# Two layers of a hybrid diffusion backbone: the feed-forward output is summed without its gate, and attention's results are divided by the row sums

## The chip, the core and the metric

The kernel runs on one core of a Trainium2 chip. The core has five engines that work side by side, each through its own queue of instructions: TensorE (matrix products, "PE" in the profile, with its weight loads as "PEld"), VectorE ("DVE"), ScalarE ("ACT"), GpSimd ("POOL") and SyncE ("SP"), which here only issues transfers between the chip's DRAM and the working memory SBUF. Matrix products are written to PSUM, a small memory of eight banks of 128 x 512 fp32. The metric is the device time of one execution in microseconds; lower is better.

## The reference

Two layers act on 128 context tokens and 512 latent tokens of width 1024 (`D`). What matters of one layer:

```python
h = layer_norm(x) * (1 + sc1) + sh1
o = concat([ssm(h), window_attention(h), head_attention(h)]) @ w_out
x = layer_norm(ALPHA * x + g1 * o, ln1_g, ln1_b)
h = layer_norm(x) * (1 + sc2) + sh2
a, gate = split(h @ w_ffn_in)
f = (silu(a) * gate) @ w_ffn_out          # inner width 2816
x = layer_norm(ALPHA * x + g2 * f, ln2_g, ln2_b)
```

`sh`, `sc` and the gates `g1`, `g2` come from a conditioning vector through a weight `w_ada`. There is one set for context rows and one for latent rows; each is a row of 1024 numbers that is the same for all rows of its kind. Attention is softmax(q k) v: window attention has 4 heads in which each latent token sees 256 nearby keys and 128 cached ones, grouped head attention has 8 query heads on 2 key heads with 640 keys.

## The kernel before, in words

The 640 rows are five tiles of 128 (tile 0 is context). Everything is fp32. The large products are made of three products of split operands: `split` makes a high part on ScalarE (L283) and the remainder on VectorE or GpSimd (L284), and `mm3` (L311 to L313) multiplies high by high, high by low and low by high. The conditioning weights are multiplied at L381.

The program is written in a framework that places every instruction. Each engine, and SyncE's one queue of transfers too, works strictly in the order of its own list. That order is laid out when the kernel is built, from the order of the source text and a modelled timeline; waits between engines are semaphores. Buffers come from named pools with a fixed number of slots: `k4` has 10 slots of 128 x 1024, `zt` has 2 of 128 x 512, and of PSUM there are two banks each for the names `psT` and `psM` and two double banks for `psS`. A transfer that waits for a slot, or for its data, holds back all transfers behind it in SyncE's queue.

*Head attention* (`gqa_units`) has, per layer, 2 key heads x 4 latent tiles x 2 pairs of query heads: 16 units (32 in all), besides the context tile. A unit has a front and a back. The front makes scores in a double bank (L1149), finds their maximum on VectorE (L1152, then times the scale, L1153), takes the exponential with its row sums on ScalarE (L1156), the reciprocal of the sums (L1158), and multiplies the 128 x 640 weights by it, on VectorE (L1160, 16 times) or GpSimd (L1162, 48 times). The back transposes the weights through `psT` (L852), copies them out (L1175), multiplies them with the values into the third `psT` bank, two heads on the two halves of the partitions (L1180), and copies the result (L1185). The front of one unit is written ahead of the back of the unit before, and pieces of other work (projections, the state-space model) are put between.

*Window attention* (`na_units`) is alike with 4 latent units per head pair, 16 in all, on 384 keys; the scaling is on VectorE 8 times and on GpSimd 24 times (L954), the value products are L976, and two backs lie behind the fronts.

*Output projection* (`wout`) handles the tiles in the groups (2, 1, 0) and (3, 4). For each tile it gates and adds the result to the old rows, which lie in a `k4` slot `xs[i]`, normalises them (`post_ln`, whose last VectorE operation is L1291), normalises again and prepares the feed-forward operands. `xs[i]` then holds the rows that the feed-forward result will be added to.

*Feed-forward* (`ffn`): the 22 blocks of 128 inner columns go in six parts of 4, 4, 4, 3, 4 and 3 blocks. For each block `ffn_in` forms seven products of 320 columns and sums them on VectorE (L1629), with weights prepared by L1579. After the blocks of a part, ten products of 128 x 512 (two column halves n, five tiles i) are made over the part's blocks, in `psM` and `psT` in turn, and summed into `xs[i]`:

```python
g = row("gp", M["gates"][1, 0]) if i == 0 else row("gs", M["gates"][1, 1])
t = ps
V.tensor_tensor(out=t, in0=ps, in1=g[:, cs], op=ALU.mult)            # L1746
```

followed in the first part by `xs = ALPHA * xs + t`, in the later ones by `xs = xs + t` (L1753), in the last with a running row sum (`residual`, L1296). The two gate rows are loaded to `k4` slots (L406) at the start of the feed-forward stage. Beside the blocks run side jobs: modulation weights of the next layer (`ada`, transfers `ev` from `w_ada`) and tables of its state-space model (`ssm_tables`, which hold further `k4` slots). After the last part the rows are normalised and, in the first layer, stored to DRAM as `xmid` (L1778).

Of the kernel before, what the change touches and what calls it, by code (L numbers as in the profile page):

```python
# [8 lines left out]
F32 = mybir.dt.float32  # L9
# [3 lines left out]
ALU = mybir.AluOpType  # L13
# [3 lines left out]
D = 1024  # L17
# [140 lines left out]
class Build:  # L158
# [689 lines left out]

    def transpose_to(self, pt, srcs):

        for j, s in enumerate(srcs):
            self.nc.tensor.transpose(pt[:, j * 128:(j + 1) * 128], s, self.ident)  # L852
# [46 lines left out]
    def na_units(self, l, N, mh, ml):  # L899
# [26 lines left out]
        def front(cb):  # L926
# [23 lines left out]
            for hh in range(2):  # L950
                if self.SCN[l][hh]:
                    V.tensor_scalar(out=P[:, hh], in0=P[:, hh], scalar1=sm[:, hh:hh + 1], scalar2=None, op0=ALU.mult)
                else:
                    G.tensor_tensor(out=P[:, hh], in0=P[:, hh], in1=sm[:, hh:hh + 1].broadcast_to([128, 384]),  # L954
                                    op=ALU.mult)
            return P

        def back(cb, P):
# [8 lines left out]
            for j in range(3):  # L967
                for hh in range(2):
# [5 lines left out]
                    else:  # L974
                        vt = vsh[:, (cb - 1) + j, hd]
                    nc.tensor.matmul(pt[hh * 64:hh * 64 + 64, 256:384], lhsT=vt, rhs=PT[:, j, hh],  # L976
                                     start=(j == 0), stop=(j == 2), tile_position=(0, hh * 64))
            a = slice(128 + cb * 128, 256 + cb * 128)
# [112 lines left out]
    def gqa_units(self, l, kv, zq, K, ss, mixd):  # L1091
# [47 lines left out]
        def front(a):  # L1139
            i, pr = a  # L1140
            qT = prepare(i)
            Ps = []
            for hh in range(2):
# [3 lines left out]
                for b in range(2):  # L1147
                    for kx, st, en in ((K["kH"], True, False), (K["kL"], False, True)):
                        nc.tensor.matmul(sp[:, b, 0:320], lhsT=qT[:, h * 128:(h + 1) * 128],  # L1149
                                         rhs=kx[kv][:, b * 320:(b + 1) * 320], start=st, stop=en)  # L1150
                nm = self.small(1, tag="gm", bufs=4)
                V.tensor_reduce(out=nm, in_=sp[:, :, 0:320], axis=AX.XY, op=ALU.max, negate=True)  # L1152
                V.tensor_tensor(out=nm, in0=nm, in1=sch, op=ALU.mult)  # L1153
                P = self.ys(n=640)
                sm = self.small(1, tag="gs", bufs=4)
                S.activation(P.rearrange("p (b k) -> p b k", b=2), sp[:, :, 0:320], AF.Exp, bias=nm, scale=sch,  # L1156
                             accum_out=sm)
                V.reciprocal(sm, sm)  # L1158
                if self.SCG[l][hh]:
                    V.tensor_scalar(out=P, in0=P, scalar1=sm, scalar2=None, op0=ALU.mult)  # L1160
                else:
                    G.tensor_tensor(out=P, in0=P, in1=sm.broadcast_to([128, 640]), op=ALU.mult)  # L1162
                Ps.append(P)
            return Ps

        def back(a, Ps):
            i, pr = a
            PT5 = self.b5()
# [16 lines left out]
            S.copy(outs[i][:, pr * 128:(pr + 1) * 128], pt[:, 256:384])  # L1185
# [256 lines left out]
    SCG = ((0, 0), (1, 0))  # L1442
    SCN = ((0, 0), (0, 1))
# [10 lines left out]
    def wout(self, l, M, mx, xsrc, nxt):  # L1454
# [6 lines left out]
        ada = self.ada_side(l, M, nxt)  # L1461
        self.function(AF.Silu, self.after)
# [7 lines left out]
        for group in self.GROUPS:  # L1470
# [23 lines left out]
            for i in group:  # L1494
# [5 lines left out]
                self.normalise(xs[i], xn, self.stats_of(xs[i], s, junk, "lsn"), self.NORMV[2])  # L1500
# [394 lines left out]
```

## Time and profile before

| | |
|---|---|
| median of 3 runs | 1859.57 us (1850.95 to 1860.01) |
| profiled execution | 1860.72 us |
| its span, first to last instruction | 1858.9 us |
| TensorE busy, share of the span | 1694.2 us, 91% |
| VectorE | 1257.5 us, 68% |
| GpSimd | 847.6 us, 46% |
| ScalarE | 820.5 us, 44% |
| mean granted TensorE clock | 0.927 of full speed |

Stages in the profiled execution, roughly: start and projections to 125 us; first layer's head attention to 350, window attention to 440, output projection to 575, feed-forward to 1000 and its end to 1090; second layer's head attention to 1215, window attention to 1340, output projection to 1425, feed-forward to the end.

How to read it: busy times are sums over instructions of an engine, and an engine that is not the last to finish can stand idle at no cost. [...] A wait is put down to the instruction that ended it.

### The profile page before, as it was taken

What the parts mean: (1) busy time and instruction counts of PE and PEld (TensorE: products, weight loads), DVE (VectorE), ACT (ScalarE), POOL (GpSimd) and SP (SyncE); (2) the same over time, 40 slices, a digit from 0 to 9 for tenths busy, and PEclk for the clock granted to TensorE, in tenths of its full rate; (3) what the DMA queues carried; (4) which work ended last, traced back from release to release, by engine and by line L of the source; (5) the groups of instructions that cost most, each with busy time, mean ns of one, the idle gap of its engine ahead of it and who ended that gap; (6) DMA issues with size and microseconds to landing.
All of it is one profiled execution on the core that took longest, in us unless ns stands there. A gap on an engine that the chain in (4) does not pass through costs nothing. (4 is left out here: it accounts for less than half of the span.)

```text
span 1858.9 us, 31182 instructions
## 1 busy us (share of the span) xinstructions
PE 1694.2 (91%) x11432; PEld 1474.2 (79%) x11432; DVE 1257.5 (68%) x2468; ACT 820.5 (44%) x1780; POOL 847.6 (46%) x723
## 2 busy tenths in 40 slices
PE   5889798899699999999997989999989999999997
PEld 3878577678498879798886978877768898998996
DVE  5466634744758876687978577665467776777777
ACT  5335444554633334242336556544565242433433
POOL 4755524237642616054456344211594473553553
PEclk9879998769799999999999999985889999999999
DMA  8534765535534554432414343453452222312312
GB/s 302 132 93 113 218 197 156 150 121 168 183 107 142 167 158 151 130 110 91 126 57 156 110 110 99 108 159 80 156 189 84 91 83 77 103 58 79 103 57 80
DMA packets 183113, 234.87 MB, mean 126 GB/s; under 512 B 78960, under 2 KB 112048, under 8 KB 182960
## 3 DMA queue, kind: packets, MB, share of 16 engines
q1 hardware_dynamic: 182960, 232.88, 41.0%
q8 instruction: 90, 1.47, 0.3%
q14 instruction: 63, 0.52, 0.1%
HBM read 203.57 MB, written 29.39 MB: 125 GB/s over the span
## 5 line engine op out<-in xcount | busy, mean ns | idle before, releaser
L284 POOL TENSOR_TENSOR wl<-wr,wh 128x512 fp32r<-128x512 f32 x362 | 507.8, 1423 | 464.9 <-ACT wh L283 313.4
L283 ACT CAST wh<-wr 128x512 fp32r<-128x512 f32 x450 | 275.3, 619 | 394.4 <-PE psM L313 101.7
L311 PE MATMUL psM<-hh,wh 128*128 128x320 f32 x560 | 180.1, 322 | 8.9 <-DVE modc L393 2.6
L312 PE MATMUL psM<-hl,wh 128*128 128x320 f32 x560 | 178.3, 318 | 0.0
L313 PE MATMUL psM<-hh,wl 128*128 128x320 f32 x560 | 178.1, 318 | 0.0
L311 PEld LDWEIGHTS psM<-hh,wh 128*128 128x128 f32 x560 | 109.1, 195 | 12.5 <-DVE modc L393 2.8
L1162 POOL TENSOR_TENSOR ys<-ys,sm 128x640 f32<-128x640 f32 x48 | 61.7, 1289 | 120.4 <-DVE sm L1158 89.4
L311 PE MATMUL psT<-hh,wh 128*128 128x320 f32 x352 | 109.8, 312 | 0.0
L313 PEld LDWEIGHTS psM<-hh,wl 128*128 128x128 f32 x560 | 108.7, 194 | 1.4 <-issue 1.4
L312 PEld LDWEIGHTS psM<-hl,wh 128*128 128x128 f32 x560 | 109.0, 195 | 1.0 <-issue 0.7
L313 PE MATMUL psT<-hh,wl 128*128 128x320 f32 x352 | 109.0, 310 | 0.0
L312 PE MATMUL psT<-hl,wh 128*128 128x320 f32 x352 | 108.9, 309 | 0.0
L230 POOL TENSOR_TENSOR sm<-sm,mhalf 128x1 f32<-128x1 f32 (+2 forms) x46 | 54.7, 1191 | 94.2 <-DVE sm L260 53.6
L1152 DVE TENSOR_REDUCE sm<-psS 128x1 f32<-128x640 f32 x64 | 52.0, 819 | 56.0 <-PE psS L1149 55.6
L1629 DVE TENSOR_TENSOR ys<-ys,psM 128x320 f32<-128x320 f32 x140 | 64.9, 481 | 34.8 <-PE psM L313 32.9
L1629 DVE TENSOR_TENSOR ys<-ys,psT 128x320 f32<-128x320 f32 x140 | 65.0, 481 | 30.4 <-PE psT L313 29.3
L311 PE MATMUL psT<-b,wh 128*128 128x320 f32 x240 | 76.9, 320 | 8.9 <-DVE ys L1629 8.9
L852 PE MATMUL psT<-ident,ys 128*128 128x128 f32 x440 | 79.3, 304 | 6.1 <-ACT sm L1185 2.0
L284 POOL TENSOR_TENSOR wl<-ws,wh 128x512 fp32r<-128x512 f32 x40 | 53.7, 1344 | 63.7 <-ACT wh L283 63.7
L311 PE MATMUL psM<-b,wh 128*128 128x320 f32 x240 | 76.6, 319 | 6.2 <-DVE ys L1629 6.2
L311 PE MATMUL psT<-wh,xs 128*128 128x512 f32 x190 | 75.8, 399 | 2.9 <-DVE k L1753 2.9
L311 PE MATMUL psM<-wh,xs 128*128 128x512 f32 x190 | 75.0, 395 | 2.5 <-DVE k L1753 2.5
(438 smaller groups left out, 5071.8 us busy)
## 6 DMA issues: line engine op xcount, KB each, us to landing
wr<-in_w_ffn_in_dram SPq DMA_DIRECT2D x88, 512.0 KB, 3.7
ev<-in_w_ada_dram SPq DMA_DIRECT2D x112, 256.0 KB, 3.8
wr<-in_w_ffn_out_dram SPq DMA_DIRECT2D x40, 512.0 KB, 3.9
wr<-in_w_out_dram SPq DMA_DIRECT2D x32, 512.0 KB, 3.7
wr<-in_w_in_dram SPq DMA_DIRECT2D x28, 512.0 KB, 4.4
wa<-in_w_ada_dram SPq DMA_DIRECT2D x24, 512.0 KB, 5.7
k<-in_x_dram SPq DMA_DIRECT2D x10, 512.0 KB, 5.9
xs<-zqk SPq DMA_DIRECT2D x32, 160.0 KB, 3.8
```

Source lines behind the costliest of these rows:

```text
L230: self.nc.gpsimd.tensor_tensor(out=o, in0=v, in1=self.mhalf.broadcast_to([128, v.shape[1]]), op=ALU.pow)
L283: nc.scalar.copy(hi, src)
L284: (lo_eng or nc.vector).tensor_tensor(out=lo, in0=src, in1=hi.bitcast(F32), op=ALU.subtract)
L311: nc.tensor.matmul(ps, lhsT=ah, rhs=bh, start=first, stop=False)
L312: nc.tensor.matmul(ps, lhsT=ah, rhs=bl, start=False, stop=False)
L313: nc.tensor.matmul(ps, lhsT=al, rhs=bh, start=False, stop=last)
L852: self.nc.tensor.transpose(pt[:, j * 128:(j + 1) * 128], s, self.ident)
L1152: V.tensor_reduce(out=nm, in_=sp[:, :, 0:320], axis=AX.XY, op=ALU.max, negate=True)
L1162: G.tensor_tensor(out=P, in0=P, in1=sm.broadcast_to([128, 640]), op=ALU.mult)
L1629: V.tensor_tensor(out=o, in0=x, in1=y, op=ALU.add)
```

## The change

Two things are changed, independent of each other.

*Feed-forward.* After the output projection's layer norm each tile's rows are also stored to DRAM (`xd`). The first part's products are copied into `xs[i]` by ScalarE, over the rows; the second to fourth parts are added without the gate. In the fifth part a block's rows come back from DRAM to a `zt` buffer, the product is added to the sum in PSUM, multiplied by the gate, and ALPHA times the rows is added. The sixth part is gated and added as before. The gate rows are asked for where the fifth part first uses them.

*Attention.* The weights are no longer scaled. After the value products a new helper, `over_sums`, makes two small products of the reciprocal sums (one column, broadcast to 64) with the identity, which puts them beside the result in the same PSUM bank, along the columns; the result is multiplied by them on VectorE. In window attention ScalarE first copies them to SBUF; in head attention the result is copied as before and then multiplied. In head attention both heads' sums lie in one tile with one reciprocal, and the scores' maximum is written to a free column of the scores' own bank. The context tile's softmax is as before.

```diff
+    def over_sums(self, pt, r):
+        for h in range(2):
+            self.nc.tensor.matmul(pt[64 * h:64 * h + 64, 384:512], lhsT=r[:, h:h + 1].broadcast_to([128, 64]),
+                                  rhs=self.ident, start=True, stop=True, tile_position=(0, 64 * h))
...
 # window attention, front
             V.reciprocal(sm, sm)
-            for hh in range(2):
-                if self.SCN[l][hh]:
-                    V.tensor_scalar(out=P[:, hh], in0=P[:, hh], scalar1=sm[:, hh:hh + 1], scalar2=None, op0=ALU.mult)
-                else:
-                    G.tensor_tensor(out=P[:, hh], in0=P[:, hh], in1=sm[:, hh:hh + 1].broadcast_to([128, 384]),
-                                    op=ALU.mult)
-            return P
+            return P, sm
...
 # window attention, back, after the value products
+            self.over_sums(pt, sm)
+            rb = self.zt(128)
+            S.copy(rb, pt[:, 384:512])
+            V.tensor_tensor(out=pt[:, 256:384], in0=pt[:, 256:384], in1=rb, op=ALU.mult)
             a = slice(128 + cb * 128, 256 + cb * 128)
             self.split(pt[:, 256:384], mh[:, a], ml[:, a])
...
 # head attention, front, for each of two heads
-                nm = self.small(1, tag="gm", bufs=4)
-                V.tensor_reduce(out=nm, in_=sp[:, :, 0:320], axis=AX.XY, op=ALU.max, negate=True)
-                V.tensor_tensor(out=nm, in0=nm, in1=sch, op=ALU.mult)
+                nm, m = self.small(1, tag="gm", bufs=4), sp[:, 0, 320:321]
+                V.tensor_reduce(out=m, in_=sp[:, :, 0:320], axis=AX.XY, op=ALU.max, negate=True)
+                V.tensor_tensor(out=nm, in0=m, in1=sch, op=ALU.mult)
...
-                V.reciprocal(sm, sm)
-                if self.SCG[l][hh]:
-                    V.tensor_scalar(out=P, in0=P, scalar1=sm, scalar2=None, op0=ALU.mult)
-                else:
-                    G.tensor_tensor(out=P, in0=P, in1=sm.broadcast_to([128, 640]), op=ALU.mult)
+                             accum_out=sm[:, hh:hh + 1])
                 Ps.append(P)
-            return Ps
+            V.reciprocal(sm, sm)
+            return Ps, sm
...
 # head attention, back, after the value products
-            S.copy(outs[i][:, pr * 128:(pr + 1) * 128], pt[:, 256:384])
+            self.over_sums(pt, sm)
+            o = outs[i][:, pr * 128:(pr + 1) * 128]
+            S.copy(o, pt[:, 256:384])
+            V.tensor_tensor(out=o, in0=o, in1=pt[:, 384:512], op=ALU.mult)
...
 # output projection, after a tile's layer norms
+                nc.sync.dma_start(xd[i], xs[i])
...
 # feed-forward
-        for key, cd in (("gp", 0), ("gs", 1)):
-            row(key, M["gates"][1, cd])
...
-                g = row("gp", M["gates"][1, 0]) if i == 0 else row("gs", M["gates"][1, 1])
-                t = ps
-                V.tensor_tensor(out=t, in0=ps, in1=g[:, cs], op=ALU.mult)
+                x = xs[i][:, cs]
                 if part == 0:
-                    V.scalar_tensor_tensor(out=xs[i][:, cs], in0=xs[i][:, cs], scalar=ALPHA, in1=t, op0=ALU.mult,
-                                           op1=ALU.add)
-                elif last:
-                    self.residual(xs[i][:, cs], t, sums[n])
+                    S.copy(x, ps)
+                elif part < len(PARTS) - 2:
+                    V.tensor_tensor(out=x, in0=ps, in1=x, op=ALU.add)
                 else:
-                    V.tensor_tensor(out=xs[i][:, cs], in0=xs[i][:, cs], in1=t, op=ALU.add)
+                    g = row("gp", M["gates"][1, 0]) if i == 0 else row("gs", M["gates"][1, 1])
+                    if last:
+                        V.tensor_tensor(out=ps, in0=ps, in1=g[:, cs], op=ALU.mult)
+                        self.residual(x, ps, sums[n])
+                    else:
+                        t = self.zt()
+                        nc.sync.dma_start(t, xd[i][:, cs])
+                        V.tensor_tensor(out=ps, in0=ps, in1=x, op=ALU.add)
+                        V.tensor_tensor(out=ps, in0=ps, in1=g[:, cs], op=ALU.mult)
+                        V.scalar_tensor_tensor(out=x, in0=t, scalar=ALPHA, in1=ps, op0=ALU.mult, op1=ALU.add)
```

## Rows read from the trace of the kernel before

**Rows 1.** The page's first section: busy us, share of the span, instructions.

```profile
PE 1694.2 (91%) x11432; PEld 1474.2 (79%) x11432; DVE 1257.5 (68%) x2468; ACT 820.5 (44%) x1780; POOL 847.6 (46%) x723
```

**Rows 2.** Stretches: us, then busy us of PE, PEld, DVE, ACT, POOL; granted clock.

```profile
125.00:350.00 225.00, 190.88 (x1651) 159.89 (x1651) 118.42 (x268) 103.59 (x259) 88.76 (x89) 0.88 0.57 165
...
575.00:1000.00 425.00, 407.08 (x2718) 360.60 (x2718) 328.44 (x563) 151.62 (x304) 188.40 (x142) 0.98 0.41 126
1090.00:1215.00 125.00, 119.01 (x969) 106.75 (x970) 86.41 (x204) 76.52 (x196) 46.64 (x50) 0.95 0.37 99
1215.00:1340.00 125.00, 118.36 (x636) 92.10 (x636) 68.42 (x152) 63.34 (x158) 33.83 (x36) 0.73 0.48 137
1425.00:1800.00 375.00, 367.16 (x2158) 340.71 (x2157) 276.67 (x421) 136.77 (x263) 175.77 (x130) 1.00 0.24 78
```

**Rows 3.** TensorE's waits, 575 to 1000 us: total us, times, longest.

```profile
PE psM L311 <- DVE ys L1629: 5.6, 5, 2.8
...
PE psT L311 <- DVE ys L1629: 3.1, 1, 3.1
PE psM L311 <- DVE k L1753: 2.5, 1, 2.5
```

**Rows 4.** TensorE's waits, 1425 to 1800 us.

```profile
PE psT L311 <- DVE ys L1629: 3.8, 5, 1.5
PE psT L311 <- DVE k L1753: 2.5, 1, 2.5
```

**Rows 5.** VectorE's groups by form: busy us, mean ns, idle us before, who ended it.

```profile
L1579 DVE TENSOR_TENSOR wr<-wr 128x512 f32<-128x512 f32 x40 | 48.0, 1200 | 0.7
...
L1746 DVE TENSOR_TENSOR psM<-psM,k 128x512 f32<-128x512 f32 x50 | 34.7, 695 | 26.9 <-PE psM L313 26.9
...
L1579 DVE TENSOR_TENSOR wr<-wr,wr 128x512 f32<-128x512 f32 x40 | 29.3, 732 | 0.9 <-POOL wl L284 0.7
...
L1753 DVE TENSOR_TENSOR k<-k,psM 128x512 f32<-128x512 f32 x40 | 27.2, 680 | 0.6
...
L1158 DVE RECIPROCAL sm<-sm 128x1 f32<-128x1 f32 x64 | 10.1, 158 | 30.8 <-ACT ys L1156 30.3
```

**Rows 6.** GpSimd's groups by form: the two scalings of attention.

```profile
L1162 POOL TENSOR_TENSOR ys<-ys,sm 128x640 f32<-128x640 f32 x48 | 61.7, 1289 | 120.4 <-DVE sm L1158 89.4 <-DVE sm L1153 13.5 <-DVE xs L740 8.2
...
L954 POOL TENSOR_TENSOR ys<-ys,sm 128x384 f32<-128x384 f32 x24 | 21.7, 921 | 70.0 <-DVE sm L949 67.9 <-PE psM L824 2.1
```

**Rows 7.** TensorE's groups by form.

```profile
L852 PE MATMUL psT<-ident,ys 128*128 128x128 f32 x440 | 79.3, 304 | 6.1 <-ACT sm L1185 2.0 <-ACT b L1175 1.3 <-DVE ys L847 1.2
...
L1149 PE MATMUL psS<-b,xs 128*128 128x320 f32 x256 | 54.1, 340 | 12.7 <-ACT ys L1156 10.7 <-DVE xs L1088 1.8
...
L1180 PE MATMUL psT<-b,b 128*64 128x128 f32 x640 | 44.7, 285 | 0.1
...
L381 PE MATMUL psM<-ev,silc 128*32 128x128 f32 x320 | 21.5, 351 | 22.2 <-DMA ev<-in_w_ada_dram 22.0
...
L976 PE MATMUL psT<-ys,k 128*64 128x128 f32 x128 | 12.5, 326 | 0.1
```

**Rows 8.** TensorE in order of time, fifth part of the first layer.

```profile
932.16 0.50 PE L311 MATMUL psM<-wh,xs 128*128 128x512 f32 x1 [2.49 <-DVE k L1753]
```

**Rows 9.** VectorE in order of time there: first and last of eight.

```profile
929.03 0.70 DVE L1746 TENSOR_TENSOR psM<-psM,k 128x512 f32<-128x512 f32 x1 [2.68 <-PE psM L313]
...
933.22 0.68 DVE L1753 TENSOR_TENSOR k<-k,psT 128x512 f32<-128x512 f32 x1
```

**Rows 10.** DMA issues by line: size and median us to landing.

```profile
k<-gates SPq DMA_DIRECT2D x8, 512.0 KB, 5.1
...
wr<-in_w_ffn_out_dram SPq DMA_DIRECT2D x8, 256.0 KB, 2.9
```

**Rows 11.** Waits of SyncE's DMA queue.

```profile
SPq L1778 <- DVE k L1291: 27.7, 4, 19.6
```

More of the change, by code (lines that the diff above doesn't have):

```diff
@@ L949, in front, with back @@
             V.reciprocal(sm, sm)
-            for hh in range(2):
-                if self.SCN[l][hh]:
-                    V.tensor_scalar(out=P[:, hh], in0=P[:, hh], scalar1=sm[:, hh:hh + 1], scalar2=None, op0=ALU.mult)
-                else:
-                    G.tensor_tensor(out=P[:, hh], in0=P[:, hh], in1=sm[:, hh:hh + 1].broadcast_to([128, 384]),
-                                    op=ALU.mult)
-            return P
-        def back(cb, P):
+            return P, sm
+        def back(cb, front):
+            P, sm = front
             PT = self.big("ys").rearrange("p (j h q) -> p j h q", j=3, h=2)
@@ L1141, in front @@
             qT = prepare(i)
-            Ps = []
+            Ps, sm = [], self.small(2, tag="gs", bufs=4)
             for hh in range(2):
@@ L1150, in front, with back @@
                                          rhs=kx[kv][:, b * 320:(b + 1) * 320], start=st, stop=en)
-                nm = self.small(1, tag="gm", bufs=4)
-                V.tensor_reduce(out=nm, in_=sp[:, :, 0:320], axis=AX.XY, op=ALU.max, negate=True)
-                V.tensor_tensor(out=nm, in0=nm, in1=sch, op=ALU.mult)
+                nm, m = self.small(1, tag="gm", bufs=4), sp[:, 0, 320:321]
+                V.tensor_reduce(out=m, in_=sp[:, :, 0:320], axis=AX.XY, op=ALU.max, negate=True)
+                V.tensor_tensor(out=nm, in0=m, in1=sch, op=ALU.mult)
                 P = self.ys(n=640)
-                sm = self.small(1, tag="gs", bufs=4)
                 S.activation(P.rearrange("p (b k) -> p b k", b=2), sp[:, :, 0:320], AF.Exp, bias=nm, scale=sch,
-                             accum_out=sm)
-                V.reciprocal(sm, sm)
-                if self.SCG[l][hh]:
-                    V.tensor_scalar(out=P, in0=P, scalar1=sm, scalar2=None, op0=ALU.mult)
-                else:
-                    G.tensor_tensor(out=P, in0=P, in1=sm.broadcast_to([128, 640]), op=ALU.mult)
+                             accum_out=sm[:, hh:hh + 1])
                 Ps.append(P)
-            return Ps
-        def back(a, Ps):
+            V.reciprocal(sm, sm)
+            return Ps, sm
+        def back(a, front):
             i, pr = a
+            Ps, sm = front
             PT5 = self.b5()
@@ L1441 @@
     XPOS = 1
-    SCG = ((0, 0), (1, 0))
-    SCN = ((0, 0), (0, 1))
     YR = 3
@@ L1461, in wout @@
         ada = self.ada_side(l, M, nxt)
+        xd = self.dp.tile([NT, 128, D], F32, name=self.nm("xd"))
         self.function(AF.Silu, self.after)
@@ L1500, in wout @@
                 self.normalise(xs[i], xn, self.stats_of(xs[i], s, junk, "lsn"), self.NORMV[2])
+                nc.sync.dma_start(xd[i], xs[i])
                 self.ffn_in_tile(xn, i, M["modc"], H)
-        return self.ffn(l, xs, M, H, nxt, ada)
+        return self.ffn(l, xs, xd, M, H, nxt, ada)
     LO = (True, True)
@@ L1705, in ffn_in_plain, with ffn @@
         yield gh, gl
-    def ffn(self, l, xs, M, H, nxt, ada):
+    def ffn(self, l, xs, xd, M, H, nxt, ada):
         nc, I = self.nc, self.I
```

## The prediction, made before the changed kernel was run

> **What bounds the kernel now.** Read the busy times first: TensorE is busy 1694.2 of 1858.9 us, VectorE 1257.5, GpSimd 847.6, ScalarE 820.5 [rows 1]. So the change, which mostly takes work from VectorE and GpSimd, can shorten the end only where TensorE stands still for them, and it adds work to TensorE itself. Then read the stretches [rows 2]. The first layer's head attention (125 to 350 us) leaves TensorE 34.1 us idle at a mean granted clock of 0.88; the second layer's (1090 to 1215) leaves 6.0. The second layer's window attention (1215 to 1340) is busy 118.4 of 125 us, but at a clock of 0.73. The feed-forward parts are nearly full: 407.1 of 425 us and 367.2 of 375, so 17.9 + 7.8 = 25.7 us idle there, at clocks of 0.98 and 1.00.
>
> Third, TensorE's waits inside these feed-forward stretches, to see who ends the idle time. Additions of the block products (L1629) end 5.6 + 3.1 us in the first layer and 3.8 in the second; the second half of the output's summing (L1753) ends 2.5 in each [rows 3, 4]. That is 17.5 us in which VectorE's lateness holds TensorE, and only 5.0 of it names the work that the change edits. Last, a close look at one of these: eight summing operations start on VectorE between 929.03 and 933.22 us, first four products with the gate, then four additions, so 4.19/7 = 0.60 us apart; a PSUM bank comes free only with an addition, and TensorE stood 2.49 us [rows 8, 9].
>
> **The change, part by part.** The sum is made against the profiled execution's own time of 1860.7 us (span 1858.9); the median of the runs shown is 1859.6, 1.1 lower, which is taken off at the end.
>
> *Summing ungated.* Each layer has ten output blocks in each of six parts. Before, each block costs a multiplication (695 ns) and an addition (680 ns) [rows 5]. Now the first part needs neither (ScalarE copies), the next three only the addition, the fifth three operations, the last two as before. In the first four parts that is 50 operations fewer per layer, in the fifth 10 more: 80 fewer in the two layers, at about 0.69 us 55 us of VectorE's 1257.5. ScalarE's 20 copies lie beside it, and that engine is idle over half the time [rows 1]. TensorE gets back what it waited for. The 2.5 us of the second layer [rows 4] stand outside the fifth part; four operations instead of eight free the bank 4 x 0.60 = 2.4 us sooner, so this wait goes. Of the 12.5 us that L1629 ends I take 5: those additions stand in VectorE's queue behind weight preparation and table work too, which stays. Term: -7.5, with bounds of 0 (all of it is other work's fault) and -15 (12.5 + 2.5).
>
> *The fifth part* now has three VectorE operations per block. Two things follow. Where four blocks are handled together, the bank is freed after the ninth operation or later rather than the fifth: 4 x 0.60 = 2.4 us more at the stall of [rows 8], and I charge the same once in each layer: +5. And the third operation needs 256 KB of the saved rows in one of two buffers; such a load lands 2.9 us after issue [rows 10]. Two buffers give a block every (2.9 + 0.7 + some 0.5 of queueing)/2, about 2.1 us, against four blocks' PSUM; close to the pace of the products themselves (12 matmuls of 512 columns), so I charge nothing more, but the upper bound is 20 loads with 1 us each: +25. Behind a load that waits for its buffer stand the weight loads of the next part on the same SyncE queue. The gate rows (512 KB, 5.1 us to landing [rows 10]) are asked for in the fifth part instead of at the start. Their two buffers are free earlier, so they can be issued far ahead; without that cover each layer pays 5.1 us once.
>
> *The stores of the rows.* Ten stores of 512 KB are new on SyncE's queue, each waiting for the layer norm on VectorE that makes its rows, with output weights, feed-forward weights and modulation weights queued behind. The kernel already has such a store: L1778 waits for the same operation (L1291), and the queue stood 27.7 us in four of them, 19.6 in the worst [rows 11]. TensorE already waits 22.0 us in all for modulation weights that come through this queue [rows 7]. The order of the queue is laid out from a modelled timeline, so most stores should stand near where their rows are ready. Term: +4 for both layers; bounds 0 and 27.7 x 10/4 = 69, of which the loads in flight should hide well over half.
>
> *Row sums after the values.* GpSimd loses 48 x 1289 ns and 24 x 921 ns = 84 us [rows 6], VectorE the other 24 scalings. On the path this is worth nearly nothing: the transposes that read the scaled weights come a unit later, and their idle time, 6.1 us over 440, names ScalarE and an earlier VectorE line, not GpSimd [rows 7]. What covers the removed scaling is the next unit's scores. New are two matmuls per unit, 64 + 32 = 96, of the same tile shape as the value products: 44.7/640 = 0.070 us each in head attention, 12.5/128 = 0.098 in window attention, so 64 x 0.070 + 32 x 0.098 = 7.6 us of TensorE. In the second layer it is full, in the first some falls into the idle time: +6. Bounds: 0, if the 34.1 us of idle time swallow it, and 96 x 79.3/440 = 17.3, if the broadcast column makes each cost what a full transpose does [rows 7]. The new copy and product after the values hold the transposes' second bank longer, but the next unit asks for it a unit later. One reciprocal per unit in place of two removes half of VectorE's stops for the exponential, 30.3 us [rows 5]; TensorE's wait on score banks is 10.7 us [rows 7]. The new product waits for a ScalarE copy on the same queue, which gives part of that back. Term: -3, bounds 0 and -10.7.
>
> [...] In the rows a 512-column operation takes 695 ns with an input in PSUM and 732 ns (mean) with both in SBUF [rows 5], so no surcharge shows and none is in the sum. [...]
>
> **Sum.** -7.5 + 5 + 4 + 6 - 3 = +4.5: 1865.2 by the profiled execution, 1864 by the median. The measurement of this kernel tells little under 0.5%, 9.3 us, from no change, so this is no change that can be told.
>
> **The rivals.** *Faster, VectorE was the hidden bound (0.27).* All 17.5 us named above but the fifth part's 2.5 go (-15), VectorE is far enough ahead in the fifth part to owe nothing, the stores hide, and the scores' wait falls by its whole 10.7 against +6: 1860.7 - 19.7, about 1840. For it: the waits named are real. Against: much of L1629's wait is work that stays, and TensorE's share is already over 95% there.
>
> *Attention gains from a quiet GpSimd (0.08).* Two forms of one line, L1579, of the same shape take 732 and 1200 ns [rows 5]: VectorE loses 0.47 us when something is in its way. Taking 72 GpSimd operations away could spare 72 x 0.47 = 34 us of VectorE and with it the full 10.7 us on the score banks: 7.7 less than the sum, 1856. [...]
>
> *Slower, SyncE's queue (0.15).* The stores stand where L1778 stands: a stop of 27.7/4 = 6.9 us each, a third of it felt by TensorE, ten times: 23 instead of 4, so 1883. It decides as soon as a store is placed several us before its rows are ready while a weight buffer is already free.
>
> *Slower, TensorE's added work (0.10).* The 96 matmuls cost 17.3 instead of 6, in stretches that run partly at the lower of the two clock levels: 1875.
>
> The forecast itself has 0.40; its own range is 1852 to 1874.
>
> **How the numbers follow.** Below 1850 lie the first rival and a little of the forecast's edge: faster 0.29. Above 1869 lie the two slower rivals and the forecast's upper edge: 0.15 + 0.10 + 0.04 = 0.29. The rest, 0.42, is within 0.5%. The range reaches into the first and third rival: 1842 to 1884.
>
> **What would show it.** Right: VectorE about 55 us less busy in the feed-forward parts and GpSimd about 84 less in attention, TensorE 6 to 9 us busier, no wait named by the summing addition outside the fifth part, a longer one inside it. Wrong: waits of TensorE for feed-forward or modulation weights right after the layer norms (the queue), idle time in the fifth part ended by loads of saved rows, or attention stretches that shrink or stretch by more than 10 us, above all with another granted clock.

## The result, and the profile after

The changed kernel takes 1840.24 us (median of 4 runs, 1836.5 to 1845.8) against 1859.62 for the kernel before on the same chip (4 runs): a ratio of 0.990, 95% interval 0.985 to 0.994. It is about 1% faster, below the range's lower end of 1842. Its profiled execution takes 1840.08 us with a span of 1837.9, against 1858.9. Ratios leave out runs more than 1.5% above the fastest of their kernel; the means of the experiments keep them, and without them a difference in that table would change by up to 6 us, a rest by about 1.

The first section of the page of the changed kernel, to be read beside [rows 1]:

```profile
PE 1675.5 (91%) x11624; PEld 1466.9 (80%) x11624; DVE 1181.7 (64%) x2380; ACT 833.4 (45%) x1816; POOL 763.4 (42%) x651
```

GpSimd lost 84.2 us, as worked out (84), and VectorE 75.8. But TensorE, which received 192 records more, is busy 18.7 us *less*. The groups of TensorE (busy us, mean ns, idle us before and who ended it) show the new products on the first line, and below it what [rows 7] showed before:

```profile
L852 PE MATMUL psT<-ident,sm 128*64 128x128 f32 x192 | 19.6, 282 | 0.0
...
L858 PE MATMUL psT<-ident,ys 128*128 128x128 f32 x440 | 75.2, 295 | 4.0 <-DVE sm L1189 2.3 <-DVE xs L1093 0.8 <-ACT ys L290 0.7
L1154 PE MATMUL psS<-b,xs 128*128 128x320 f32 x256 | 54.7, 345 | 8.5 <-ACT ys L1160 6.6 <-DVE xs L1093 1.8
L1181 PE MATMUL psT<-b,b 128*64 128x128 f32 x640 | 43.7, 283 | 2.0 <-ACT b L1176 1.9
```

The 96 products have 192 records in the trace, two each, and take 19.6 us, 0.204 each. So work was added, and yet the busy time fell. The windows by stage say how: the kernel before first, cut at the first scores of each kind of attention, then the changed kernel (columns as in [rows 2]; the last but two is the granted clock).

```profile
125.00:337.00 212.00, 180.13 (x1609) 152.12 (x1609) 109.51 (x245) 96.75 (x241) 88.61 (x88) 0.90 0.56 161
337.00:430.00 93.00, 88.04 (x459) 65.81 (x458) 47.63 (x115) 47.70 (x124) 31.22 (x34) 0.75 0.46 137
1086.00:1238.00 152.00, 140.26 (x1148) 124.79 (x1148) 102.98 (x231) 89.68 (x225) 53.25 (x58) 0.96 0.40 108
1238.00:1338.00 100.00, 96.80 (x454) 73.59 (x455) 51.44 (x123) 49.26 (x127) 26.41 (x27) 0.66 0.46 135
```

```profile
125.00:325.00 200.00, 173.05 (x1676) 148.60 (x1676) 101.49 (x245) 96.10 (x241) 48.52 (x56) 0.94 0.60 174
325.00:417.00 92.00, 88.33 (x477) 68.44 (x477) 46.77 (x121) 48.84 (x131) 17.16 (x18) 0.76 0.44 131
560.00:985.00 425.00, 402.53 (x2681) 358.57 (x2682) 300.07 (x504) 156.12 (x310) 184.12 (x140) 0.98 0.42 131
1076.00:1235.00 159.00, 146.27 (x1230) 130.93 (x1230) 92.47 (x225) 91.62 (x233) 34.07 (x43) 0.95 0.40 108
1235.00:1318.00 83.00, 80.24 (x458) 60.39 (x458) 43.59 (x110) 46.91 (x125) 17.15 (x18) 0.82 0.52 152
1402.00:1780.00 378.00, 372.08 (x2198) 345.16 (x2197) 258.30 (x390) 146.24 (x281) 178.27 (x132) 1.00 0.26 83
```

In these two executions two stages carry the gain. The first layer's head attention is 12 us shorter, of which 4.9 are idle time (31.9 to 27.0) and the rest goes with a clock of 0.94 instead of 0.90. The second layer's window attention is 17 us shorter without doing less: its clock is 0.82 instead of 0.66. TensorE's busy time there fell from 96.8 to 80.2 us, with 458 records for 454. Against this stand 7 us more in the second layer's head attention and 3 between the first layer's window attention and it.

Only the first of the two is stable. The changed kernel was profiled twice more (e5, span 1818.6 us; e18, 1845.0); these are its two window attentions, cut alike:

```profile
323.00:407.00 84.00, 80.67 (x476) 61.89 (x476) 46.02 (x120) 48.50 (x131) 17.17 (x18) 0.84 0.48 144
1219.00:1301.00 82.00, 79.24 (x455) 59.77 (x454) 42.73 (x108) 46.84 (x125) 17.15 (x18) 0.82 0.52 152
```

```profile
319.00:421.00 102.00, 95.51 (x476) 73.88 (x477) 46.50 (x120) 49.18 (x131) 17.15 (x18) 0.70 0.41 120
1233.00:1326.00 93.00, 90.69 (x455) 68.63 (x455) 42.38 (x107) 47.52 (x125) 17.14 (x18) 0.70 0.44 134
```

Between these two executions of one program lie 29 us in window attention alone, where the clock was lower, so a single profile can't show what the edit did to the clock of this stage. The first layer's head attention took 200, 198 and 195 us in the three.

Inside the feed-forward the terms can be read one by one. TensorE in order of time, fifth part of the first layer, as in [rows 8]:

```profile
918.54 0.80 PE L311 MATMUL psT<-wh,xs 128*128 128x512 f32 x1 [4.88 <-DVE k L1761]
```

2.49 us before, 4.88 now: the 2.4 us of four more operations. TensorE's waits in the two feed-forward stretches (560 to 985, then 1402 to 1780 us), as in [rows 3, 4]; L1633 is what L1629 was:

```profile
PE psT L311 <- DVE k L1761: 4.9, 1, 4.9
PE psM L311 <- DVE ys L1633: 4.8, 4, 2.7
PE psT L311 <- DVE ys L1633: 4.3, 2, 3.1
```

```profile
PE psT L311 <- DVE ys L1633: 2.9, 5, 0.8
PE psM L311 <- DVE ys L1633: 1.1, 1, 1.1
PE psT L311 <- DVE k L1761: 0.9, 1, 0.9
```

The second layer's 2.5 us by the summing addition are gone (0.9 is left in its fifth part). L1633 holds TensorE for 4.8 + 4.3 + 2.9 + 1.1 = 13.1 us. Before, L1629 held it 12.5 us by the lines of [rows 3, 4] and 13.9 in all, since the second layer's stretch (1425 to 1800 us) has one line more:

```profile
PE psM L311 <- DVE ys L1629: 1.4, 2, 1.1
```

VectorE's summing groups show that this work did shrink. The edited lines, of which these are some, take 96.4 us in all where they took 151.2, the 55 us less of the forecast:

```profile
L1750 DVE TENSOR_TENSOR k<-psT,k 128x512 f32<-128x512 f32 x30 | 20.7, 690 | 31.9 <-PE psT L313 31.9
L1750 DVE TENSOR_TENSOR k<-psM,k 128x512 f32<-128x512 f32 x30 | 20.7, 689 | 28.5 <-PE psM L313 28.5
...
L1761 DVE SCALAR_TENSOR_TENSOR k<-zt,psT 128x512 f32<-128x512 f32 x10 | 6.8, 682 | 2.4 <-DMA zt<-xd 2.3
```

The transfers of the saved rows (all instructions on `xd`, who waited for them, and their time to landing):

```profile
L1758 SPq DMA_DIRECT2D zt<-xd x20: 319/320/432, 485.1 to 1764.7; - x20
L1504 SPq DMA_DIRECT2D xd<-k x10: 319/326/433, 440.8 to 1383.9; - x10
its engine sat idle before it (us, times) until:
who waited for it (us, times):
  DVE k L1761: 2.3, 2
...
DMA to landing us min/median/max: 2.4/2.9/5.6
```

Twenty loads cost VectorE 2.3 us, and no engine waited for a store. SyncE's queue did stand at both, most of all

```profile
SPq L1758 <- DVE k L1761: 37.3, 16, 10.7
SPq L1504 <- DVE b L284: 11.8, 2, 6.4
```

in all 48.4 us at the loads, mostly for a `zt` buffer, and 17.4 at the stores. Little of it reached TensorE: the modulation weights `ev` that come through the same queue hold it 27.4 us (22.2 and 5.2 in two banks) for 25.8 before (22.0 and 3.8), and 24.4 in e2, which has the same stores.

### The profile page after: what moved, and what is told of

Read it like the earlier page. It is cut to its first block, busy times and chain, and to the rows that moved or that the text cites. A ratio compares the mean times of both kernels' runs of the same rounds, so it can differ in the third digit from the quotient of the medians.

```text
span 1837.9 us, 31442 instructions
## 1 busy us (share of the span) xinstructions
PE 1675.5 (91%) x11624; PEld 1466.9 (80%) x11624; DVE 1181.7 (64%) x2380; ACT 833.4 (45%) x1816; POOL 763.4 (42%) x651
## 4 chain that ended last, share of the span: by engine, by line
PE 64%; DVE 13%; DMA 11%; POOL 4%; ACT 4%; issue 3%; SPq 1%; POOLq 0%; DVEq 0%; ACTq 0%
PE psM L311 8%; PE psM L312 8%; PE psM L313 8%; PE psT L311 5%; PE psT L312 5%; PE psT L313 5%; DMA ev<-in_w_ada_dram 3%; PE psT L858 3%; POOL wl L284 2%; DMA wr<-in_w_ffn_in_dram 2%; PE psS L767 2%; PE psS L311 2%; PE psS L312 2%; PE psS L313 2%; PE psS L1154 2%
## 5 line engine op out<-in xcount | busy, mean ns | idle before, releaser
L311 PEld LDWEIGHTS psM<-hh,wh 128*128 128x128 f32 x560 | 108.1, 193 | 10.7 <-DVE modc L391 3.6
L1583 DVE TENSOR_TENSOR ws<-wr,wr 128x512 f32<-128x512 f32 x40 | 33.6, 839 | 85.8 <-DMA wr<-in_w_ffn_in_dram 54.4
L1633 DVE TENSOR_TENSOR ys<-ys,psM 128x320 f32<-128x320 f32 x140 | 64.9, 482 | 35.4 <-PE psM L313 33.5
L1157 DVE TENSOR_REDUCE psS<-psS 128x1 f32<-128x640 f32 x64 | 52.0, 826 | 54.6 <-PE psS L1154 51.8
L1633 DVE TENSOR_TENSOR ys<-ys,psT 128x320 f32<-128x320 f32 x140 | 64.9, 481 | 29.7 <-PE psT L313 28.6
L858 PE MATMUL psT<-ident,ys 128*128 128x128 f32 x440 | 75.2, 295 | 4.0 <-DVE sm L1189 2.3
L311 PE MATMUL psM<-wh,hh 128*128 128x256 f32 (+1 forms) x232 | 73.1, 315 | 5.9 <-DVE sm L1326 2.9
```

Of the source, the lines that this page charges most:

```text
L311: nc.tensor.matmul(ps, lhsT=ah, rhs=bh, start=first, stop=False)
L1157: V.tensor_reduce(out=m, in_=sp[:, :, 0:320], axis=AX.XY, op=ALU.max, negate=True)
L1583: V.tensor_tensor(out=o, in0=x, in1=y, op=op)
L1633: V.tensor_tensor(out=o, in0=x, in1=y, op=ALU.add)
```

## The experiments

Every run lists its span and TensorE's mean granted clock. In the traces this clock is 1.00 of full speed or 0.50: in windows of 2 us of the profile before, all fifteen from 370 to 400 us have 0.50 and all ten from 402 to 422 us have 1.00, and a value between the two (0.83 from 400 to 402 us) stands where a window holds a change. So the time at the lower level is twice the span times one minus the mean clock. Within one kernel, whose instructions are the same each time, the span follows the clock: over 279 runs of 18 kernels (the changed one in three sets), each set taken from its own mean, the slope is -13.3 us for +0.01 of clock (standard error 0.5, correlation -0.88). A mean clock 0.01 higher means about 37 us less at the lower level (2 x 0.01 x 1856), so each of these is worth 13.3/37 = 0.36 us. By the clock of 0.50 alone it would be at most a half, as an estimate; the runs give less, and their number is used here.

With this slope each kernel's mean difference from the kernel before is split into what goes with its clock and a rest. The split takes for granted that the slope within a kernel also holds from kernel to kernel, which no run tests. The table gives the ratio to the kernel before on the same chip, then means over all runs; the rest is good to 1 or 2 us.

| kernel | runs | ratio [95%] | span | clock | difference | by clock | rest |
|---|---|---|---|---|---|---|---|
| before, five chips | 111 | | 1855.6 | 0.929 | | | |
| changed | 4 | 0.990 [0.985, 0.994] | 1838.5 | 0.940 | -17.1 | -14.7 | -2.5 |
| changed, e5 | 6 | 0.981 [0.977, 0.986] | 1826.2 | 0.944 | -29.5 | -20.1 | -9.4 |
| changed, e18 | 9 | 0.989 [0.985, 0.992] | 1837.9 | 0.938 | -17.7 | -11.7 | -6.0 |
| e1 attention | 10 | 0.991 [0.988, 0.994] | 1837.7 | 0.939 | -17.9 | -12.7 | -5.2 |
| e2 feed-forward | 12 | 0.995 [0.992, 0.998] | 1846.3 | 0.934 | -9.3 | -6.0 | -3.3 |
| e3 window attention | 12 | 0.997 [0.994, 1.000] | 1847.3 | 0.937 | -8.4 | -10.1 | +1.8 |
| e4 head attention | 11 | 0.994 [0.990, 0.997] | 1842.4 | 0.932 | -13.2 | -4.2 | -9.1 |
| e6 window, products only | 12 | 0.995 [0.992, 0.998] | 1844.7 | 0.938 | -11.0 | -11.7 | +0.7 |
| e7 window, no scaling | 12 | 0.994 [0.992, 0.997] | 1844.5 | 0.937 | -11.1 | -10.3 | -0.8 |
| e8 changed, bank free sooner | 6 | 0.990 [0.985, 0.994] | 1838.1 | 0.941 | -17.5 | -15.0 | -2.5 |
| e9 idle operations, window | 12 | 0.999 [0.996, 1.001] | 1854.2 | 0.931 | -1.5 | -2.0 | +0.6 |
| e10 window, products 3 times | 8 | 0.991 [0.988, 0.994] | 1840.6 | 0.942 | -15.0 | -16.7 | +1.6 |
| e11 head, products only | 6 | 0.988 [0.985, 0.992] | 1835.1 | 0.942 | -20.5 | -16.3 | -4.2 |
| e12 head, no scaling | 6 | 0.978 [0.975, 0.981] | 1815.0 | 0.941 | -40.7 | -15.9 | -24.8 |
| e13 idle operations, head | 6 | 0.990 [0.986, 0.994] | 1843.9 | 0.928 | -11.7 | +1.9 | -13.5 |
| e14 idle operations x3, window | 12 | 1.001 [0.998, 1.004] | 1856.9 | 0.928 | +1.3 | +1.2 | +0.1 |
| e15 changed + idle operations | 12 | 0.991 [0.988, 0.994] | 1841.1 | 0.938 | -14.5 | -11.0 | -3.5 |
| e16 feed-forward + head products | 6 | 0.984 [0.980, 0.987] | 1825.5 | 0.947 | -30.1 | -24.1 | -6.0 |
| e17 feed-forward + idle, head | 6 | 0.988 [0.985, 0.992] | 1834.5 | 0.933 | -21.1 | -4.6 | -16.5 |

Several expectations speak of span x clock; it is the coarser form of the same split, since it counts a microsecond at the lower level as a half.

**Which half?** e1 and e2 take the attention half and the feed-forward half of the diff alone; e3 and e4 take window attention's and head attention's part of e1.

```diff
 # e1: window and head attention as changed, feed-forward as before
 # e2: feed-forward as changed, attention as before
 # e3: window attention alone as changed
 # e4: head attention alone as changed
```

> The attention half of the change alone; feed-forward as before. Theory A (the gain is attention's: with the scaling gone the units follow each other sooner and TensorE runs less time at its lower clock): 18 to 23 us faster than before, about 1839, time at the lower clock well under the 272 us of before. Theory B (the gain is VectorE's relief in the feed-forward parts): no gain, 0 to 8 us slower for the 96 added matmuls, 1860 to 1868.

> The feed-forward half alone (rows stored to DRAM, ungated sum, fifth part with three operations); attention as before. Theory A: within 5 us of before, with a longer stall in the fifth part and stops at the saved rows' loads. Theory B: 12 to 20 us faster, 1840 to 1848.

> Only window attention divides after the values. Theory A, if the second layer's window attention is where it came from (99 us before, 83 after): 12 to 17 us faster, 1843 to 1848, with that stretch near 83 us. If that shortening came from elsewhere (the order that the head attention leaves, or which stretch falls to the lower clock by chance): within 5 us of before. Theory B: 0 to 4 us slower.

> Only head attention divides after the values. Theory A: first layer 13 us shorter, second 7 longer, as in the full change: about 6 us faster, 1854. If the order of the work decides more than the edit: up to 15 us either way. Theory B: 0 to 5 us slower.

All four are faster than before, e3 barely, so no single piece holds the gain, and in e1, e2 and e3 most of it goes with the clock. Only in e4 is the rest the larger part. e1 came out as its theory A has it, at the lower end; e2 and e3 lie between their two theories, and e4 gained twice what its theory A has, within the 15 us that it leaves to the order.

**The change again, and the fifth part's bank freed after one operation.** e5 is the changed kernel, e8 writes the fifth part's first sum to SBUF, over `x`, so that the bank waits for one operation instead of three:

```diff
-                        V.tensor_tensor(out=ps, in0=ps, in1=x, op=ALU.add)
-                        V.tensor_tensor(out=ps, in0=ps, in1=g[:, cs], op=ALU.mult)
-                        V.scalar_tensor_tensor(out=x, in0=t, scalar=ALPHA, in1=ps, op0=ALU.mult, op1=ALU.add)
+                        V.tensor_tensor(out=x, in0=ps, in1=x, op=ALU.add)
+                        V.tensor_tensor(out=x, in0=x, in1=g[:, cs], op=ALU.mult)
+                        V.scalar_tensor_tensor(out=x, in0=t, scalar=ALPHA, in1=x, op0=ALU.mult, op1=ALU.add)
```

> The changed kernel once more, for its median and its mean clock beside the kernels of this batch. The runs so far say that span times mean clock is 1724 us before and 1729 changed, so the whole gain would be the clock: expected 1836 to 1843 at a mean clock near 0.940 against 0.929. If attention (18 us) and feed-forward (9 us) simply added up, it would be 1829.

> The changed kernel, but in the fifth part the first operation writes the sum to the rows' place in SBUF and the other two work there, so a PSUM bank is free after one operation. If the 4.9 us stall of TensorE in the first layer's fifth part is the nine operations of three blocks each: the stall falls below 1 us there, and the kernel is 4 to 9 us faster than the changed one. If the saved rows' loads hold it: no change.

In e8 the summing operations of the fifth part hold TensorE for 4.2 us in all, none longer than 1.5:

```profile
PE psM L311 <- DVE k L1759: 2.9, 2, 1.5
PE psT L311 <- DVE k L1759: 1.3, 1, 1.3
```

The 4 to 9 us expected did not come (0.990, e5 beside it 0.981): a stall of 4.9 us is less than these kernels differ by other causes. e5 itself was expected at 1836 to 1843 and has a median of 1822, with a clock of 0.944.

**Window attention: the products without the edit, and the edit without the products.** e6 keeps the scaling and adds the pair of products, whose result nobody reads. e7 drops the scaling and puts nothing in its place, so that window attention's result stays undivided. e10 is e6 with the pair made three times.

```diff
 # e6, in back, the scaling kept (e10: three times)
+            self.over_sums(pt, sm)
             a = slice(128 + cb * 128, 256 + cb * 128)
 # e7: as changed, without
-            self.over_sums(pt, sm)
-            rb = self.zt(128)
-            S.copy(rb, pt[:, 384:512])
-            V.tensor_tensor(out=pt[:, 256:384], in0=pt[:, 256:384], in1=rb, op=ALU.mult)
```

Where the expectations write C and L: C is the theory that TensorE's added work holds its clock up, L that the shorter way from scores to values does it.

> The kernel before with the scaling kept, and in window attention the two small products per unit added, their result unused: TensorE work alone. Theory C (TensorE is granted the higher level more because it is given more to do in window attention): mean clock up by about 0.007 as in the run with window attention changed alone, time at the lower level about 30 us less, and 5 to 10 us faster than before although 6 us of work came in. Theory L (earlier results, not more work, raise the clock): clock as before (0.929), 4 to 8 us slower.

> The kernel before without the scaling in window attention and without anything in its place; the results stay undivided. Theory L: the shorter chain packs TensorE's work, mean clock 0.937 or more and 12 to 16 us faster. Theory C: clock as before or lower, 0 to 4 us faster.

> The kernel before, scaling kept, with the pair of products of the sums made three times in each window attention unit (their results are not used). Time at full clock (span x mean clock) should be 3 x 6.5 = 19 us above before's 1724, so about 1743, by every theory. If added TensorE work is what raised the clock with one pair (0.930 to 0.938), three pairs raise it to about 0.95 and the time is about 1830 to 1840, no slower than with one pair. If one pair's gain came from the placing, the clock is anywhere between 0.930 and 0.940 and the time 1854 to 1874.

Adding work gains 11.0 us and taking work away gains 11.1, each as much as the edit that does both (8.4) and each by the clock alone. So neither C nor L is the cause by itself. Three pairs give a little more clock than one (0.942, where C expected about 0.95) and cost TensorE three times the work; the rest, +1.6, shows almost none of the 14.1 us that the 96 products take in e10's trace. The coarser span times clock is 9.1 us above before's, so how much of their price is hidden depends on the split.

**Head attention, the same two.** e11 keeps the scaling and adds unused products (with eight slots for the sums instead of four); e12 drops both the scaling and the division (its result stays undivided).

```diff
 # e11, in back, the scaling kept
+            self.over_sums(pt, sms)
             S.copy(outs[i][:, pr * 128:(pr + 1) * 128], pt[:, 256:384])
 # e12: as changed, without
-            self.over_sums(pt, sm)
             S.copy(o, pt[:, 256:384])
-            V.tensor_tensor(out=o, in0=o, in1=pt[:, 384:512], op=ALU.mult)
```

> The kernel before, scaling kept, with the pair of products of the sums in each head attention unit, unused. The work alone costs 64 pairs at 4 records of 0.204 us / 2, so 13 us, some of it in the first layer's idle time. If head attention's edit gained through its missing scaling, this one loses: span x clock 1730 to 1737, and 1862 to 1869 at before's clock of 0.930. If TensorE's added work raises the clock by filling it, or if any new placing does, the clock is 0.935 or more and the time 1845 to 1858.

> The kernel before, in whose head attention the weights are not scaled and the result is not divided by the row sums either (that part of the computation is left out). Against the edit of head attention alone (span x clock 1717.7, mean 1842) it saves the two products, the copy's follower and their waits: if the missing scaling is the gain and the products its price, span x clock falls by another 8 to 13 to about 1705 to 1710 and the time is 1828 to 1835. If the edit's gain was placing, span x clock stays near 1718 to 1724 and the time at 1840 to 1855.

e11 was expected to lose if the missing scaling was the gain; it gains 20.5 us, as much as the whole change, from products that nobody reads. e12 is the fastest of all at 1815, faster than any theory had it. From e12 to e4 the products and the division cost 27.4 us; from before to e11 nearly the same products gain 20.5. Prices of single edits do not add here.

**A new placing and nothing else.** Any edit makes the framework lay out the order of all later instructions anew. These kernels multiply a small tile by 1 and change no other instruction: e9 once and e14 three times in each window attention unit, e13 in each head of head attention; e15 does what e9 does, to the changed kernel.

```diff
 # e9 (e14: three times; e15: in the changed kernel)
-            V.reciprocal(sm, sm)
+            V.reciprocal(sm, sm); V.tensor_scalar(out=sm, in0=sm, scalar1=1.0, scalar2=None, op0=ALU.mult)
 # e13
-                V.tensor_tensor(out=nm, in0=nm, in1=sch, op=ALU.mult)
+                V.tensor_tensor(out=nm, in0=nm, in1=sch, op=ALU.mult); V.tensor_scalar(out=nm, in0=nm, scalar1=1.0, scalar2=None, op0=ALU.mult)
```

> The kernel before with 16 extra VectorE operations of 128 x 2 in window attention, which multiply the reciprocal sums by 1; no work is moved or saved, but the order of all later work is laid out anew. If the placing alone decides TensorE's clock, the mean granted clock rises as in the two earlier variants of window attention, from 0.930 to about 0.937, and the time falls to about 1845 (ratio 0.994). If what raised the clock there was their added products or their missing scaling, clock and time stay as before: 0.930, ratio 0.999 to 1.003.

> [...] If any new placing raises the clock, the mean clock is 0.935 to 0.942 and the time 1838 to 1850; if it takes an edit that adds or removes real work, 0.928 to 0.932 and 1856 to 1862.

> The kernel before with three idle operations of 128 x 2 in each window attention unit instead of one. If a larger shift of the placing is enough, the clock is 0.935 to 0.940 as in the two earlier variants of window attention and the time about 1845; if it takes real work, 0.929 to 0.932 and 1854 to 1859.

> The changed kernel with 16 idle operations of 128 x 2 in window attention. If its clock of 0.940 to 0.944 belongs to the edit, it stays there, with a time of 1822 to 1842. If it belongs to the placing, it can be anything from 0.929 up, and a time of 1845 to 1858 is as likely as not.

In window attention these two new placings change neither time nor clock (e9, e14), and the changed kernel keeps most of its clock under one (e15). In head attention it takes 11.7 us off without touching the clock (e13), which no expectation had: 64 added operations, each 148 ns in its trace (the same operation on 128 x 1, L244, has a mean of 146 ns in the profile before), and the kernel is faster. Where, the windows and TensorE's waits in e13's first head attention show:

```profile
124.00:324.00 200.00, 177.66 (x1608) 150.80 (x1609) 112.29 (x275) 96.59 (x241) 89.41 (x88) 0.90 0.59 172
...
1219.00:1321.00 102.00, 98.51 (x459) 73.79 (x460) 50.32 (x122) 48.29 (x125) 27.02 (x28) 0.67 0.44 134
```

```profile
PE psS L767 <- DVE k L753: 1.5, 2, 0.8
```

The first layer's head attention is 12 us shorter at before's clock of 0.90: TensorE's idle time fell from 31.9 to 22.3. The second layer's window attention stays at 0.67. One wait stands out. The kernel before had, in the same stage,

```profile
PE psS L767 <- DVE k L753: 6.3, 2, 5.5
PE psS L1149 <- ACT ys L1156: 6.2, 3, 2.3
```

and the changed kernel has

```profile
PE psS L1154 <- ACT ys L1160: 2.8, 2, 2.3
...
PE psS L767 <- DVE k L753: 1.7, 1, 1.7
```

L767 is a product of the state-space model, which is placed between the units of attention and which neither kernel edits. So 4.6 us less waiting in this stage belong to a neighbour that now stands elsewhere, and an idle operation moves it as well as the edit does.

Every kernel was profiled, and this stage, cut the same way, falls into two groups. It takes 207 to 212 us in before, e2, e3, e6, e7, e9, e10, e11, e14 and e16, and 192 to 202 in the three profiles of the changed kernel and in e1, e4, e8, e12, e13, e15 and e17. The second group holds every kernel that dropped the scaling in head attention and both that put the idle operations there. e11 and e16, whose unused products also bring a new order and whose wait at L767 fell too (4.0 and 2.6 us), stay at 210. So this part of the gain comes back in every profile of the changed kernel, and some new orders give it without the edit, though not all.

**What is left for the attention half?** e17 joins e13's idle operations to the feed-forward half, with attention's work as before; e16 joins e11's unused products to it; e18 is the changed kernel beside e17 on one chip.

```diff
 # e17 = e2 + e13;  e16 = e2 + e11;  e18 = the changed kernel
```

> The feed-forward half of the change together with the unused products of the sums in head attention, whose scaling is kept. If the two gains add (9 and 20 us), the time is about 1826 and the clock 0.945; if both gain the same thing, a clock near 0.942, the time is 1833 to 1840.

> The feed-forward half of the change, and in attention only the 64 idle operations of 128 x 1. If the attention half gains by the new placing alone, this kernel is as fast as the changed one, 1825 to 1842. If the missing scaling is worth something of its own, it is no faster than the feed-forward half alone, 1846 to 1852.

> The changed kernel again, beside the kernel above. On two chips its ratio was 0.990 and 0.981; between 0.980 and 0.992 is expected by every theory.

e17 is as fast as the changed kernel on the same chip, 0.988 against 0.989, as was expected if the attention half gains by a new placing. But it gets there by the other way: its clock is 0.933 and nearly all its gain is rest. e16, whose added products nobody reads, has the highest clock (0.947) and, after e12, which leaves work out, the lowest mean, 1825.5; but e5's runs of the changed kernel have 1826.2 on another chip, so a kernel that beats the changed one is not shown.

## Why the prediction was wrong, step by step

**The failed step is the sum: it has no term for TensorE's clock.** It took the clocks of [rows 2] as given, 0.88 in the first layer's head attention and 0.73 around the second layer's window attention, and named "another granted clock" only as what would make it wrong. Over the changed kernel's 19 runs the mean span is 1834.3, 21.3 below before's; 15.0 of this go with the mean clock, which rises from 0.929 to 0.940. The rest is -6.3, where +4.5 was forecast. Where in the kernel this clock was gained the profiles do not settle: the second layer's window attention had 0.66 before, and 0.82, 0.82 and 0.70 in three profiles of the changed kernel. That time goes with the clock within one kernel is shown by the runs of each; that the edit's variants have a higher clock than before is shown by e1 to e3, e6, e7 and e10 to e12 (0.934 to 0.942; e4, 0.932, is the weak one) beside 0.928 to 0.931 in three kernels that were only placed anew.

**Ungated sum (-7.5).** VectorE's work shrank as forecast, and the second layer's 2.5 us went. The other 5 did not: L1633's waits are 13.1 us for 13.9 (the prediction's 12.5 left out a line of 1.4). Its lower bound, that this is other work's fault, was nearly right for them. The *fifth part (+5)* was exact where it could be read, 4.88 for 2.49; the second layer's copy of it was 0.9, and e8 shows that the time hardly notices. The *stores (+4)* were nearer to nothing: the queue stood 17.4 us at them, but TensorE waits only 1.6 us more for the modulation weights `ev`, and in e2 not at all. Together the three terms are +1.5; e2 gives a rest of -3.3 and 6.0 by the clock.

**Matmuls (+6).** Mis-sized: a unit has ten value products, 32 units have 320, and L1180 has 640 records [rows 7], so a product has two, and the forecast took one record's 0.070 us for a whole product. The products took 19.6 us of TensorE's time, above the bound of 17.3. Even so their price is not seen: e6, e10 and e11 show rests of +0.7, +1.6 and -4.2 for 32, 96 and 64 of them. Only from e12 to e4 do they cost anything, 15.7 us of rest together with the division.

**Score waits (-3).** The wait on score banks went from 10.7 to 6.6 us, about as forecast. What was missed is that a new order moves other work too: e13 has a rest of -13.5 for no saving at all, so e4's -9.1 and e12's -24.8 can't be put down to the missing scaling alone. This is the second thing that the sum has no term for, and the part that every profile of the changed kernel repeats: its first head attention takes 195 to 200 us, where the kernels of the other group take 207 to 212.

**The rivals.** *VectorE the hidden bound* gave 1840, the time that came, by luck: its -15 needed L1629's waits to vanish, and 13.1 us of them are still there. *Quiet GpSimd*: the slow form of L1579 went from 1200 to 1118 ns, but its four forms together only from 146.2 to 144.4 us, where this rival had 34 less, and no run singles out GpSimd as what slows it. The wait of the scores fell by 4.1 us, and GpSimd's load is untouched in e6, e11 and e13, which gain 11.0, 20.5 and 11.7 us without it. *SyncE's queue* and *TensorE's added work* did not come; e11 is the reverse of the second. The product that follows the maximum has a median of 159 ns with both inputs in SBUF (before) and of 152 ns with the maximum in PSUM (after; min, median and longest ns):

```profile
L1153 DVE TENSOR_TENSOR sm<-sm,sm x64: 132/159/1234, 128.0 to 1216.9; 128x1 f32<-128x1 f32 x64
L1158 DVE TENSOR_TENSOR sm<-psS,sm x64: 136/152/159, 128.4 to 1209.3; 128x1 f32<-128x1 f32 x64
```

So an input in PSUM shows no surcharge in this product either, and the sum rightly has none.

**What stays open.** Why edits that add products, and edits that only remove the scaling, both raise the clock, when both together in head attention (e4) hardly do and when three times the products raise it little more. The amount of TensorE's work alone does not explain it. A new placing did not raise the clock in the three kernels that were only placed anew, but every edit brings an order of its own, and three orders are few: that the particular order decides remains a rival. One profile for each kernel, whose clock differs from run to run, is too little to find what precedes each fall: the profiled execution of e6, a kernel with a mean clock of 0.938, had 0.930, and 0.63 in the second layer's window attention, while that of e9, with a mean of 0.931, had 0.79 there. What part of head attention's rest belongs to the missing scaling is open too: to tell it, the order would have to be held fixed.

## What to carry to other kernels

Where TensorE runs part of a stage at its lower level, as here in attention with mean clocks of 0.66 to 0.96, a forecast needs a term for its clock, with a range for both signs, and should read idle time and clock stage by stage before it adds up microseconds of instructions. Before a stage's clock is called an effect of the edit, profile the same kernel several times. Where a framework lays out the order anew at every edit, run a control that changes only the order, in the same place as the edit: here sixty-four idle operations gave about half of the change's mean gain (11.7 of 21.3 us). Count the records of one product before a record's mean duration is taken for its price.

## What the runs showed of the hardware that was not expected

In the profile before, TensorE spent about 271 us at its lower level (2 x 0.073 x 1858.9). The two window attentions, a tenth of the span, hold about 114 of them (2 x 0.25 x 93 + 2 x 0.34 x 100), although TensorE is 95 and 97% busy there by its records; the two head attentions, a fifth of the span, hold about 55 (2 x 0.10 x 212 + 2 x 0.04 x 152), although the first leaves it more idle time (180.1 of 212 us busy). Part of that busy time is the lower level itself: the 455 records of the second one kept TensorE busy 79.2 us at 0.82 in e5 and 90.7 us at 0.70 in e18. The same kernel on one chip is granted another clock from run to run (e4: 0.925 to 0.940, 1859.1 us at the first, 1832.9 at the second), so that 26 us lie between two runs of one program. And 64 added matrix products (e11), or 64 added idle operations (e13), made a kernel faster by 1%.
